# Layer 1's output projection: which matmul of the late rows is two columns wider

## The chip, the cores and the metric

One core of one Trainium2 chip runs the whole program. The metric is the device time of one execution in microseconds (us). The kernel before takes 564.82 us, the median of three runs (564.3 to 565.0).

## The reference

The model is a trunk of two layers over one sequence of 256 tokens, 1024 wide. Layer 0 mixes tokens with multi-head latent attention, layer 1 with block attention of 8 heads of 128 and a relative bias. Each mixer is followed by a dense MLP, 1024 to 4096 to 1024, with a squared ReLU. All is float32.

```
x = x + mixer(rms_norm(x, attn_norm[i]))       # ends in out @ w_o, 1024 x 1024
h = rms_norm(x, mlp_norm[i])
x = x + (relu(h @ w_in) ** 2) @ w_out
```

What the change touches is the product of the attention's result with `w_o` in layer 1. It changes no number of the output: the columns that it adds to a matmul are written to a part of a PSUM bank that nothing reads.

## The kernel before, in words

Every dense product is made of three matmuls in a row. A weight tile of 128 x 1024 float32, a *unit*, comes in by DMA (`raw`), ScalarE rounds it to a tile `wh` (line 169), and VectorE subtracts to get the rest `wl` (line 178). The activations are split the same way: `hTh` and `hTl` ahead of the MLP, `a[0]` and `a[1]` between its two products, and `aT[0]` and `aT[1]` for the heads. `mm3` (line 87) then issues three products into one PSUM bank: first `wh` with the upper half of the activations (i = 0), second `wl` with the same upper half (i = 1), third `wh` with the lower half (i = 2). In each of them the weights are the stationary 128 x 128 block and the activations are the moving 256 columns. In the trace these show as `ps<-hTh,wh`, `ps<-hTh,wl`, `ps<-hTl,wh`; for heads (`aT`) and for the second MLP product (`a`) buffer numbers are left out, so that the first and third product are both `aT,wh` or `a,wh`, and the second is `aT,wl` or `a,wl`.

`mm3` takes an argument `wide`. With it the first product of the three goes to 258 columns in place of 256. `wider` (line 103) makes the two longer access patterns; the two more columns are the first two of the next tile of activations, and they land in columns 256 and 257 of the bank, which hold nothing else. `other_type` (line 107) wraps the places inside the MLP at which matmuls of another kind stand between the products (a float32 sum over partitions, the bf16 sums of the bias tables). The next `first` or output row after such a place has a wide first product (lines 922 and 970).

`run_heads` (line 618) writes out by hand the order of one layer's attention: logits, transposes and value products of the 8 heads between the projections. Output rows 0 to 3 of `w_o` (128 output columns each) are built up head by head in `o` (line 626). Output rows 4 to 7, the late ones, are made by `col` (line 640). Row 4 is built in pieces between the heads, and its last pieces come after `o(6)` as heads 4, 5, 6 (counted from 0), then `o(7)`, then head 7; rows 5, 6, 7 follow in one go, 24 products each. Then the MLP begins: `first` (line 914) makes 8 groups of 48 products from `hTh` and `hTl`, output rows of 48 products follow, and the same again for the second half of the hidden units. `mid` is None in layer 0 and a function in layer 1; `col` uses it to tell the layers apart.

In layer 0 the wide products are those of row 4 with heads 0 and 5 (`d == 4 and h in (0, 5)`). In layer 1 there is one, that of row 5 with head 0 (`(d, h) == (5, 0)`). All of these are first products. Later in either layer's MLP there is one float32 sum over partitions inside the seventh group of 48 (line 953), after its 44th product, and the eighth group begins with a wide product. In layer 0 there are also the bias tables' sums inside the output rows; layer 1 has none.

All matmuls stand in one queue, in program order. The DMAs are issued by SyncE.

Of the kernel before, what the change touches and what calls it, by code (L numbers as in the profile page):

```python
# [18 lines left out]
P = 128  # L19
# [4 lines left out]
S = 256  # L24
NT = S // P
KD = D // P
H = 8
# [33 lines left out]
def trunk(ctx: ExitStack, tc: tile.TileContext, A, out):  # L61
# [9 lines left out]
    def ps():  # L71
        return psum.tile([P, 512], F32, name="ps", tag="ps")
# [11 lines left out]
    def mm(o, a, b, start, stop):  # L84
        nc.tensor.matmul(o, a, b, start=start, stop=stop)  # L85

    def mm3(o, a, b, start, stop, wide=None, between=None):

        for i, (w, t) in enumerate(((0, 0), (1, 0), (0, 1))):
            if wide and i == 0:  # L90
                mm(wide[0], a[w], wide[1], start, False)
            else:
                mm(o, a[w], b[t], start and i == 0, stop and i == 2)
            if between and between[0] == i:
                between[1]()
# [4 lines left out]

    moved = [True]

    def wider(bank, b):
        moved[0] = True
        return bank[:, :S + 2], flat(b[:, :2])[:, :S + 2]

    def other_type(i, f):
        def run():
# [5 lines left out]
    def flat(ap):  # L114
        return ap.rearrange("p a b -> p (a b)")
# [45 lines left out]
    def hi(n=1, eng=nc.scalar):  # L161

        for _ in range(n):
            i = len(his)
            if i < min(used[0] + RING, len(units)):
                load_raw()
                w = units[i][1]
                his.append(wsp.tile([P, 1024], F32R, name="wh", tag="wh"))
                (eng.copy if eng is nc.scalar else eng.tensor_copy)(his[i][:, :w], raws[i][:, :w])  # L169

    def lo(n=1, eng=nc.vector):

        for _ in range(n):
            i = len(los)
            if i < len(his):
                w = units[i][1]
                los.append(wsp.tile([P, 1024], F32R, name="wl", tag="wl"))
                eng.tensor_sub(los[i][:, :w], raws[i][:, :w], f32(his[i][:, :w]))  # L178
                load_raw()

    def fill(n=1):
        lo(n)
        hi(n)
# [7 lines left out]
    def unit(i):  # L191
        while len(his) <= i:
            hi()
        while len(los) <= i:
            lo()
        return his[i], los[i]

    def done(i):

        used[0] = max(used[0], i + 1)  # L200

    def part(u, sl):
        return u[0][:, sl], u[1][:, sl]
# [82 lines left out]
    class SumSquares:  # L286


        def __init__(self):
            self.tot = work.tile([P, 2, S], F32, name="ssum", tag="ssum", bufs=1)  # L290
            self.prev = None
# [38 lines left out]
    class Norm:  # L330
# [19 lines left out]
        def rows(self, tok):  # L350
            self.y = t2(self.nh, self.width)
            nc.vector.scalar_tensor_tensor(self.y, self.p.rearrange("p (a b) -> p a b", b=self.width), tok,
                                           self.rs[:, :, None].to_broadcast([P, self.nh, self.width]),
                                           op0=OP.mult, op1=OP.mult)
# [189 lines left out]
    def head_tiles(l):  # L544

        cm = ExitStack()
        pool = cm.enter_context(tc.tile_pool(name=f"heads{l}", bufs=1))
        r = []
        for c in range(2):
            r.append({n: pool.tile([P, *sh], F32, name=f"{n}{c}")  # L550
                      for n, sh in (("k", (HG, S)), ("q", (HG, S)), ("v", (NT, HG, P)))})
        room(pool, f"aT{l}")
        aT = [pool.tile([P, H, S], F32R, name=f"aT{i}") for i in range(2)]
        return cm, r, aT

    class Head:


        def __init__(self, hd, aT, h, bias, extra=None):
            self.aT = (aT[0][:, h], aT[1][:, h])  # L560
            self.two = aT[0][:, h:h + 2] if h < H - 1 else None
            self.i = h % HG
            self.hd = hd[h // HG]
            self.h, self.bias, self.extra = h, bias, extra
# [28 lines left out]
        def turn(self):  # L593
            pt = ps()
            for i in range(3):
                nc.tensor.transpose(pt[:, i * P:(i + 1) * P], self.p[:, i * P:(i + 1) * P], ident)  # L596
            self.pT = work.tile([P, 3 * P], F32, name="pT", tag="pT", bufs=3)
            nc.scalar.copy(self.pT, pt[:, :3 * P])
# [15 lines left out]
    def out_residual(a, d, gname):  # L614
        nc.vector.tensor_add(x[:, d], a, x[:, d])
        make_h_filled(d, gname)

    def run_heads(hs, proj, post, rows, turn, mid, base, gname, n1):

        A_ = [h.logits for h in hs]  # L620
        W_ = [h.weights for h in hs]
        B_ = [h.turn for h in hs]
        C_ = [h.values for h in hs]
        accs = []

        def o(h, ds=range(4)):
            u = unit(base + h // 2)
            for d in ds:
                if h == 0:
                    accs.append(ps()[:, :S])  # L630
                c = (h % 2) * 512 + d * P
                mm3(accs[d], part(u, slice(c, c + P)), hs[h].aT, h == 0, h == H - 1)
                if h == H - 1:
                    out_residual(accs[d], d, gname)
            if h % 2:
                done(base + h // 2)

        late = {}

        def col(d, hh):  # L640
            if d not in late:
                late[d] = ps()
            u = unit(base + d)
            for h in hh:

                wide = d == 4 and h in (0, 5) if mid is None else (d, h) == (5, 0)
                mm3(late[d][:, :S], part(u, slice(h * P, (h + 1) * P)), hs[h].aT, h == 0, h == H - 1,
                    wider(late[d], hs[h].two) if wide else None)
            if hh[-1] == H - 1:
                done(base + d)  # L650
                out_residual(late[d][:, :S], d, gname)

        if mid is not None:
            proj("k1", 0)
            fill(n1)
            post("k1", 0)
            mid()
            proj("k1", 1)
            lo(n1)
            rows("k1", 0)  # L660
            hi(n1)
            post("k1", 1)
        A_[0]()
        proj("v1", 0)
        if mid is not None:
            lo(n1)
            rows("k1", 1)
        W_[0]()
        hi(n1)
        post("v1", 0)  # L670
        turn("k1", 0)
        A_[1]()
        if mid is None:
            rows("k1", 1)
        B_[0]()
        proj("v1", 1)
        lo(n1 + (mid is None))
        W_[1]()
        hi(n1)
        post("v1", 1)  # L680
        turn("k1", 1)
        C_[0]()
        A_[2]()
        B_[1]()
        proj("q1", 0)
        lo(n1)
        W_[2]()
        hi(n1)
        post("q1", 0)
        C_[1]()  # L690
        A_[3]()
        B_[2]()
        proj("q1", 1)
        lo(n1)
        W_[3]()
        rows("q1", 0)
        hi(n1)
        post("q1", 1)
        C_[2]()
        B_[3]()  # L700
        o(0)
        fill()
        turn("q1", 0)
        rows("q1", 1)
        C_[3]()
        o(1)
        fill()
        turn("q1", 1)
        o(2, range(2))
        A_[4]()  # L710
        o(2, range(2, 4))
        W_[4]()
        A_[5]()
        lo()
        o(3)
        B_[4]()
        hi()
        W_[5]()
        A_[6]()
        col(4, [0, 1])  # L720
        C_[4]()
        B_[5]()
        W_[6]()
        A_[7]()
        lo()
        col(4, [2, 3])
        C_[5]()
        B_[6]()
        hi()
        W_[7]()  # L730
        o(4)
        fill()
        C_[6]()
        B_[7]()
        o(5)
        fill()
        C_[7]()
        o(6)
        fill()
        col(4, [4, 5, 6])  # L740
        o(7)
        col(4, [7])
        for d in range(5, KD):
            col(d, range(H))
# [91 lines left out]
    heads_ctx, hd, aT = head_tiles(0)  # L836
# [16 lines left out]
    for o, a, b in rope_halves(m[:, :, 0], m[:, :, 1]):  # L853
        a, b = (i[:, :, None, :].to_broadcast([P, NT, 2, HALF]) for i in (a, b))
# [46 lines left out]
    def mlp(l, base, fillers, inside, finish):  # L901

        with tc.tile_pool(name=f"mlp{l}", bufs=1) as pool:
# [10 lines left out]
            def first(b, r, j, split_k, between=None):  # L914
# [3 lines left out]
                for f, k in [(f, k) for k in range(KD) for f in range(2)] if split_k else \  # L918
                        [(f, k) for f in range(2) for k in range(KD)]:
                    c = (k % 4) * 256 + f * P  # L920
                    wide = None
                    if k == f == 0 and not moved[0]:
                        wide = wider(p[f], hTh)
                    mm3(o[f], part(u[k // 4], slice(c, c + P)), hT(k), k == 0, k == KD - 1, wide,
                        between if (f, k) == (1, KD - 2) else None)
# [326 lines left out]
```

## Time and profile before

| | us |
|---|---|
| median of three runs | 564.82 |
| the profiled execution | 564.11 |
| its span, first to last instruction | 562.3 |
| TensorE busy in it | 557.0 (99%) |
| VectorE busy | 394.7 (70%) |
| ScalarE busy | 302.4 (54%) |
| GpSimd busy | 90.5 (16%) |

The profile is of one execution. The span leaves out 1.8 us around the first and last instruction. A busy TensorE is one that has some matmul in flight: a matmul's duration as shown is 0.28 us, but the next one begins about 0.12 us after it began, so the pace has to be read from start times and not from busy time or durations. Times inside the trace are us from the start of the span.

### The profile page before, as it was taken

The page shows a single profiled execution, that of the slowest core. Times are in us where ns is not written, and L with a number is a line of the kernel's source. Part 1 is how long each engine was busy: PE and PEld are TensorE (multiplying, and loading weights), DVE is VectorE, ACT ScalarE, POOL GpSimd, SP SyncE. Part 2 cuts the span into 40 slices and gives each one's busy share as a digit, 9 for nine tenths or more (in the row PEclk, how much of TensorE's full clock was granted, in tenths as well). Part 3 has the DMA queues.
Part 4 walks back from the last instruction along what each step waited for, and adds up shares of the span by engine and source line. Part 5 has one row for each costly group of instructions (what it writes and reads, how often), then busy time and mean ns, then how long its engine had stood idle before and what let it go on. Part 6 is the DMA issues. An engine that isn't in the chain of part 4 may idle for free.

```text
span 562.3 us, 11331 instructions
## 1 busy us (share of the span) xinstructions
PE 557.0 (99%) x4612; PEld 543.8 (97%) x4612; DVE 394.7 (70%) x654; ACT 302.4 (54%) x495; POOL 90.5 (16%) x108
## 2 busy tenths in 40 slices
PE   8999999999999999999999999999999999999997
PEld 6878999999999999999999999999999999999997
DVE  5897777778997689766566657776767554777530
ACT  6899675765443355433555466756655333555310
POOL 4792100041231000011231201000211110000100
PEclk9999999999999999999999999999999999999999
DMA  8834445686566376546528344455756763765800
GB/s 300 305 113 120 144 143 160 190 273 188 191 203 207 113 223 190 188 150 194 176 82 277 119 167 145 132 170 168 268 172 195 221 187 108 219 195 155 279 26 29
DMA packets 29188, 99.60 MB, mean 177 GB/s; under 512 B 3824, under 2 KB 4720, under 8 KB 29136
## 3 DMA queue, kind: packets, MB, share of 16 engines
q1 hardware_dynamic: 28656, 97.94, 54.4%
q0 software_dynamic: 336, 0.92, 0.4%
q8 instruction: 36, 0.59, 0.4%
q14 instruction: 16, 0.13, 0.1%
q10 hardware_dynamic: 144, 0.02, 0.0%
HBM read 97.82 MB, written 1.05 MB: 176 GB/s over the span
## 4 chain that ended last, share of the span: by engine, by line
PE 96%; DVE 1%; DMA 1%; SPq 1%; issue 0%; ACT 0%; DVEq 0%
PE ps L85 93%; PE ps L372 1%; DMA x<-in_xT 1%; PE ps L596 1%; DVE wl L178 1%; SPq L158 0%; SPq L230 0%; PE ps L512 0%; DVE hTl L280 0%; ACT wh L169 0%; ACT hTh L279 0%; SPq L234 0%; DVE t L1066 0%; DVE rr L408 0%; PE ps L882 0%
## 5 line engine op out<-in xcount | busy, mean ns | idle before, releaser
L178 DVE TENSOR_TENSOR wl<-raw,wh 128x1024 fp32r<-128x1024 f32 x177 | 218.5, 1250 | 37.2 <-ACT wh L169 36.7
L169 ACT CAST wh<-raw 128x1024 fp32r<-128x1024 f32 x177 | 182.1, 1045 | 71.3 <-PE ps L85 53.6
L85 PE MATMUL ps<-a,wh 128*128 128x256 f32 x1024 | 178.5, 278 | 0.0
L85 PEld LDWEIGHTS ps<-a,wh 128*128 128x128 f32 x1024 | 155.7, 188 | 0.0
L85 PE MATMUL ps<-a,wl 128*128 128x256 f32 x512 | 143.0, 279 | 0.0
L85 PE MATMUL ps<-hTl,wh 128*128 128x256 f32 x512 | 142.7, 279 | 0.0
L85 PE MATMUL ps<-hTh,wl 128*128 128x256 f32 x512 | 142.6, 278 | 0.0
L85 PE MATMUL ps<-hTh,wh 128*128 128x256 f32 x512 | 142.4, 278 | 0.0
L85 PEld LDWEIGHTS ps<-hTh,wh 128*128 128x128 f32 x512 | 96.3, 188 | 0.1
L85 PEld LDWEIGHTS ps<-hTl,wh 128*128 128x128 f32 x512 | 96.2, 188 | 0.1
L85 PEld LDWEIGHTS ps<-a,wl 128*128 128x128 f32 x512 | 96.2, 188 | 0.0
L85 PEld LDWEIGHTS ps<-hTh,wl 128*128 128x128 f32 x512 | 96.1, 188 | 0.0
L933 ACT ACTIVATE t<-ps 128x512 f32<-128x512 f32 (+1 forms) x34 | 19.5, 573 | 66.5 <-PE ps L85 66.3
L85 PE MATMUL ps<-aT,wh 128*128 128x256 f32 x256 | 50.7, 289 | 0.0
L935 DVE SCALAR_TENSOR_TENSOR t<-ps,t 128x512 f32<-128x512 f32 (+1 forms) x34 | 22.4, 659 | 39.5 <-ACT t L933 39.5
L85 PE MATMUL ps<-wh,hTh 128*128 128x256 f32 (+2 forms) x224 | 45.7, 289 | 0.5 <-DVE wh L446 0.5
L85 PE MATMUL ps<-wl,hTh 128*128 128x256 f32 (+2 forms) x224 | 45.0, 285 | 0.4 <-DVE wl L178 0.4
L85 PE MATMUL ps<-wh,hTl 128*128 128x256 f32 (+2 forms) x224 | 45.0, 285 | 0.0
L85 PEld LDWEIGHTS ps<-aT,wh 128*128 128x128 f32 x256 | 40.5, 188 | 0.2
L85 PE MATMUL ps<-aT,wl 128*128 128x256 f32 x128 | 35.8, 280 | 0.0
L85 PEld LDWEIGHTS ps<-wh,hTh 128*128 128x128 f32 x224 | 34.4, 188 | 1.1 <-ACT hTh L279 1.0
L85 PEld LDWEIGHTS ps<-wl,hTh 128*128 128x128 f32 x224 | 34.5, 188 | 1.0 <-DVE wl L178 0.9
(167 smaller groups left out, 619.3 us busy)
## 6 DMA issues: line engine op xcount, KB each, us to landing
raw<-in_w_in_mlp SPq DMA_DIRECT2D x64, 512.0 KB, 4.3
raw<-in_w_out_mlp SPq DMA_DIRECT2D x64, 512.0 KB, 4.3
raw<-in_w_qkv SPq DMA_DIRECT2D x24, 512.0 KB, 4.2
raw<-in_w_u SPq DMA_DIRECT2D x8, 512.0 KB, 5.8
win<-in_w_in SPq DMA_DIRECT2D x8, 352.0 KB, 5.2
raw<-in_w_o0a SPq DMA_DIRECT2D x4, 512.0 KB, 3.9
raw<-in_w_o0b SPq DMA_DIRECT2D x4, 512.0 KB, 3.6
raw<-in_w_o1a SPq DMA_DIRECT2D x4, 512.0 KB, 4.2
```

Of the source, the lines that this page charges most:

```text
L85: nc.tensor.matmul(o, a, b, start=start, stop=stop)
L169: (eng.copy if eng is nc.scalar else eng.tensor_copy)(his[i][:, :w], raws[i][:, :w])
L178: eng.tensor_sub(los[i][:, :w], raws[i][:, :w], f32(his[i][:, :w]))
L372: nc.tensor.transpose(pt[:, i * P:(i + 1) * P], yf[:, i * P:(i + 1) * P], ident)
L596: nc.tensor.transpose(pt[:, i * P:(i + 1) * P], self.p[:, i * P:(i + 1) * P], ident)
L933: nc.scalar.activation(rl, src, AF.Relu)
L935: nc.vector.scalar_tensor_tensor(sq, src, 0.0, rl, op0=OP.max, op1=OP.mult)
```

## The change

`mm3` can now make any of its three products the wide one; `wider` takes the product's number. In layer 0 nothing changes. In layer 1 the wide first product of row 5 with head 0 goes back to 256 columns; row 4 gets a wide first product with head 0 and a wide third product with head 5. The wide one of head 0 begins the accumulation in the two extra columns, that of head 5 adds to them. The third product takes its moving columns from `aT[1]` (the lower half), the others from `aT[0]`.

```
     def mm3(o, a, b, start, stop, wide=None, between=None):
         for i, (w, t) in enumerate(((0, 0), (1, 0), (0, 1))):
-            if wide and i == 0:
-                mm(wide[0], a[w], wide[1], start, False)
+            if wide and i == wide[2]:
+                mm(wide[0], a[w], wide[1], start and i == 0, stop and i == 2)
             else:
                 mm(o, a[w], b[t], start and i == 0, stop and i == 2)
...
-    def wider(bank, b):
+    def wider(bank, b, which=0):
         moved[0] = True
-        return bank[:, :S + 2], flat(b[:, :2])[:, :S + 2]
+        return bank[:, :S + 2], flat(b[:, :2])[:, :S + 2], which
...
-            self.two = aT[0][:, h:h + 2] if h < H - 1 else None
+            self.two = [a[:, h:h + 2] for a in aT] if h < H - 1 else None
...
-                wide = d == 4 and h in (0, 5) if mid is None else (d, h) == (5, 0)
-                mm3(late[d][:, :S], part(u, slice(h * P, (h + 1) * P)), hs[h].aT, h == 0, h == H - 1,
-                    wider(late[d], hs[h].two) if wide else None)
+                wide = None
+                if d == 4 and h in (0, 5):
+                    which = 2 if h and mid is not None else 0
+                    wide = wider(late[d], hs[h].two[which // 2], which)
+                mm3(late[d][:, :S], part(u, slice(h * P, (h + 1) * P)), hs[h].aT, h == 0, h == H - 1, wide)
```

## Rows read from the trace of the kernel before

**Rows 1.** The page: span, and busy us, share and instructions of the engines.

```profile
span 562.3 us, 11331 instructions
...
PE 557.0 (99%) x4612; PEld 543.8 (97%) x4612; DVE 394.7 (70%) x654; ACT 302.4 (54%) x495; POOL 90.5 (16%) x108
```

**Rows 2.** Chain of waits in order of time, its end: start, us, engine, instructions.

```profile
362.96 196.15 PE ps L85 x1662
...
559.13 0.42 DVE t L1066
```

**Rows 3.** Timeline of TensorE, layer 0's late rows: start us, duration, operation, count.

```profile
82.00 0.28 PE L85 MATMUL ps<-aT,wl 128*128 128x256 f32 x1
...
82.35 0.28 PE L85 MATMUL ps<-aT,wl 128*128 128x256 f32 x1
82.47 0.40 PE L85 MATMUL ps<-aT,wh 128*128 128x256 f32 x2
82.70 0.28 PE L85 MATMUL ps<-aT,wl 128*128 128x256 f32 x1
...
83.05 0.28 PE L85 MATMUL ps<-aT,wl 128*128 128x256 f32 x1
...
130.76 0.59 PE L85 MATMUL ps<-ssum,ones 128*128 128x256 f32 x2
```

**Rows 4.** Timeline of TensorE in layer 0's MLP, 131 to 148 us.

```profile
131.31 0.28 PE L85 MATMUL ps<-hTh,wh 128*128 128x256 f32 x1
...
131.66 0.28 PE L85 MATMUL ps<-hTh,wh 128*128 128x258 f32 x1
...
147.43 0.34 PE L85 MATMUL ps<-parts,st 128*128 128x96 bf16 x4
```

**Rows 5.** Timeline of TensorE, layer 1: late rows and MLP, 355 to 559 us.

```profile
355.92 0.47 PE L85 MATMUL ps<-aT,wh 128*128 128x256 f32 x1
356.39 0.39 PE L85 MATMUL ps<-aT,wl 128*128 128x256 f32 x1
...
366.87 0.40 PE L85 MATMUL ps<-aT,wh 128*128 128x256 f32 x2
...
369.23 0.28 PE L85 MATMUL ps<-aT,wl 128*128 128x256 f32 x1
...
369.59 0.28 PE L85 MATMUL ps<-aT,wl 128*128 128x256 f32 x1
...
416.70 0.59 PE L85 MATMUL ps<-ssum,ones 128*128 128x256 f32 x2
...
417.60 0.28 PE L85 MATMUL ps<-hTh,wh 128*128 128x258 f32 x1
...
558.81 0.28 PE L85 MATMUL ps<-a,wh 128*128 128x256 f32 x1
```

**Rows 6.** Line 85 from 81 to 82.58 us: durations min/median/max in ns.

```profile
L85 PEld LDWEIGHTS ps<-aT,wl x5: 187/188/193, 80.8 to 82.2; 128*128 128x128 f32 x5
L85 PE MATMUL ps<-aT,wl x5: 280/281/281, 80.9 to 82.3; 128*128 128x256 f32 x5
```

**Rows 7.** The same from 378 to 416 us, where the three products have three names.

```profile
L85 PE MATMUL ps<-hTh,wh x108: 279/281/281, 377.9 to 415.8; 128*128 128x256 f32 x108
L85 PEld LDWEIGHTS ps<-hTh,wl x108: 186/187/188, 378.0 to 415.8; 128*128 128x128 f32 x108
...
L85 PEld LDWEIGHTS ps<-hTl,wh x108: 187/188/189, 378.1 to 415.9; 128*128 128x128 f32 x108
```

**Rows 8.** The same from 365 to 369 us.

```profile
L85 PEld LDWEIGHTS ps<-aT,wl x12: 186/187/192, 364.9 to 368.8; 128*128 128x128 f32 x12
```

**Rows 9.** The same from 450 to 558 us.

```profile
L85 PE MATMUL ps<-hTh,wl x128: 279/281/281, 468.6 to 513.5; 128*128 128x256 f32 x128
```

**Rows 10.** Busy time by stretch: PE, PEld, DVE, ACT, POOL; clock, DMA share, GB/s.

```profile
84.00:130.00 46.00, 46.00 (x409) 46.00 (x408) 34.71 (x48) 29.81 (x43) 7.28 (x7) 1.00 0.64 205
...
450.00:500.00 50.00, 50.00 (x427) 50.00 (x426) 30.80 (x35) 22.05 (x27) 2.95 (x4) 1.00 0.58 177
```

## The prediction

> **What bounds the kernel now.** I read the engines' shares first: TensorE is busy 99% of the span, the next engine (VectorE) 70% [rows 1]. The chain of waits comes second, read at its end: one unbroken piece of TensorE, 196.15 us and 1662 matmuls long from 362.96 us, and behind it a last addition and the store [rows 2]. So from 363 us on nothing sets the end but how fast TensorE goes from one matmul to the next. The change lies at the head of that piece. The third view is the timeline of TensorE, and it has to be read by starts. In layer 0 the second products (`aT,wl`) of neighbouring groups of three start at 82.00 and 82.35 us, and a little later at 82.70 and 83.05; over a long stretch one sees two different paces:
>
> - *Fast*: from 82.70 us to the sum at 130.76 us there are by the code 2 + 3 products (row 4's heads 5 and 6), 12 (`o(7)`), 3 (row 4's head 7), 72 (rows 5 to 7), 6 x 48 and 44 of the MLP, so 424 starts: 48.06 us / 424 = 113.4 ns [rows 3]. From the wide product at 131.66 to the bias sums at 147.43 us there are 48 + 48 + 43 = 139: 15.77 / 139 = 113.5 ns [rows 4].
> - *Slow*: from the third product of row 4's head 5, the first of the two in the row of 366.87, to the sum at 416.70 there are 1 + 3 + 12 + 3 + 72 (row 4's rest, `o(7)`, rows 5 to 7), 288 and 44, so 423: 49.83 / 423 = 117.8 ns. From 417.60 to the last matmul at 558.81 there are 48 + 8 x 48 + 8 x 48 + 8 x 48 - 1 = 1199: 141.21 / 1199 = 117.8 ns [rows 5].
>
> The shape is the same 128 x 256 everywhere, the granted clock is 1.00 in both layers, and TensorE never sits idle in either [rows 10]. Layer 0's MLP runs at 113.4 ns, layer 1's at 117.8 ns, and nothing in the arithmetic asks for it.
>
> **What switches the pace.** In layer 0 the two matmuls in the row of 82.47 are the third product of row 4's head 4 and the wide first product of head 5. Up to it groups of three are 0.35 to 0.36 us apart; from 82.70 on 113.4 ns is held over 48 us, through the late rows and into the MLP [rows 3]. The wide product at 131.66, behind the float32 sum, is again followed by the fast pace, while the three starts just ahead of it, from 131.31, took 0.35 us [rows 4]. In layer 1 the wide product of row 5, 19 starts behind that of 366.87 and so at 369.1 us, is followed by the slow pace; so is the one at 417.60 [rows 5]. So a wide product can lift the pace, and sometimes doesn't.
>
> The line view says when. In the slow pace the three products of a group aren't alike. From 378 to 416 us one has the longest weight load (up to 189 ns: `hTl,wh`, the third), the next one the longest matmul (median 281: `hTh,wh`, the first), the one after it the shortest load (median 187, from 186: `hTh,wl`, the second) [rows 7]. This order of three can begin at any product: from 450 to 558 us the median of 281 is on `hTh,wl` [rows 9]. In layer 0, just before the wide product that works, the second product carries the 281 and loads of 188 [rows 6]; so the one before it, the first, carries the long load, and there the wide one sits. In layer 1, ahead of the wide one that fails, the second carries the load of 187 [rows 8]; so the third carries the long load, and the wide one sits on the first, a step too late. My reading: two more columns lift the pace when they fall on the product of the long load. The change moves them in layer 1 to a third product of that same stretch.
>
> **The change part by part.**
>
> - *Row 4, head 0, wide first product.* Two more columns: by TensorE's pace of 113.4 ns for 256 columns under 1 ns, and the matmul it falls on is followed by a start 0.47 us later, where 0.12 is usual (355.92 to 356.39) [rows 5]. It waits there for its `wl`, so the columns are covered; without that cover they cost 1 ns. Nothing else comes of it: a wait and three heads' transposes stand between it and the last stretch.
> - *Row 5, head 0, wide product removed.* Back to 256 columns: under 1 ns.
> - *Row 4, head 5, wide third product.* Under 1 ns itself. If it lifts the pace, 423 starts, from 366.87 to 416.70, go at 113.4 ns: 49.83 - 423 x 0.1134 = 49.83 - 47.97 = 1.86 us less.
> - *The sum at 416.70 and the wide first product at 417.60.* Neither is edited. The sum drops the pace in layer 0 too (0.35 us for three starts from 131.31 [rows 4]), and there the same order of matmuls, which came in at the fast pace, is lifted by its wide product at 131.66. Layer 1 came in slow. If it now comes in fast, I take it to be lifted as layer 0 is: 141.21 - 1199 x 0.1134 = 141.21 - 135.97 = 5.24 us less.
> - *What a faster TensorE asks of the others.* Weights must come 4% sooner. Layer 0's MLP does that with the same tiles: at the fast pace DVE 34.71, ACT 29.81 of 46 us and 205 GB/s, no idle time of TensorE; layer 1's 450 to 500 has less to do (30.80, 22.05 of 50 us) [rows 10]. The last matmul to the end of the span, 3.5 us (558.81 to 562.3), stays.
>
> No instruction, DMA or wait is added or moved past a queue; only three matmuls change their columns. What the trace doesn't show is a wide third product. Below, it can do what the failing one of row 5 did: nothing that lasts, and one group of 0.36 us behind it (369.23 to 369.59) in place of 0.353 [rows 5], which rival 4 prices. Above, what the working ones did: 7.10 us. I take the upper end, since it stands on the product on which the working one stood.
>
> Sum: 1.86 + 5.24 = 7.10 us. The profiled execution took 564.11, so 557.0 for it; the median of the runs shown is 0.7 above that execution, so 557.7 for a median. I forecast 557.6.
>
> **A rule of the Trainium skill against it.** *TensorE: Matmul & The Clock Gate*, "Back-to-back issue gap", gives the isolated gap of a warm matmul by its columns alone, N/2.4 + 2.5 ns; by it 256 columns take 109.2 ns, two more 0.8, and the change is worth nothing: 564.8. This trace disagrees, with 113.4 and 117.8 ns at one shape and one clock. The same section says that in a stream the spacing comes from load and matmul together; the rows agree, but it doesn't say which pace one gets.
>
> **Rivals.**
>
> 1. *The columns lift nothing in layer 1.* Then both stretches stay at 117.8 ns: 564.8. Either they cost their columns alone and layer 0's fast pace has another reason (against it: the pace turns at both wide products of rows 3 and 4, within a group). Or the order of the three is another one in the changed kernel, so that the third product is the wrong one. For it: the order can begin at any product. Against: the stretch behind the last transposes has the same matmuls as before up to the wide one, and from 365 to 416 us the second product kept the short load [rows 7, 8].
> 2. *The first lifts, the second doesn't.* The pace falls at the sum and stays: 564.8 - 1.9 = 562.9. For it: 417.60 failed before. Against: layer 0's twin.
> 3. *The first fails, the second happens to lift* from another order: 564.8 - 5.2 = 559.6. It needs a shift that nothing here calls for.
> 4. *Slower: the wide product puts the stream on a third, slower pace.* Behind the failing wide product one group takes 0.36 us, 120 ns a start, 2.2 more than the slow pace (369.23 to 369.59) [rows 5]. Held over 423 + 1199 starts it would cost 1622 x 2.2 = 3.6 us: 568.4. It decides from 0.7 ns a start over these 1622, which is 1.1 us. Against: over the 1199 starts behind 417.60 the mean is 117.8, so no such pace lasted there.
>
> **How the numbers follow.** Forecast 0.70, rival 1 0.16 (0.04 by its first cause, 0.12 by its second), rival 2 0.07, rival 3 0.03, rival 4 0.04. The forecast's own range is 556.6 to 558.6 (the spread of the runs, 0.7, and some 0.3 for the entries into the pace). For 8 in 10 the range takes in rivals 3 and 2: 556.4 to 563.2. A measurement of this kernel can tell 0.2% (1.1 us) from no change. Faster by more: 0.70 + 0.07 + 0.03 = 0.80; within: 0.16; slower: 0.04.
>
> **What would show it.** In the profile after, second products behind 367.1 us 0.34 us apart in place of 0.353; the sum at about 414.8 in place of 416.70; the wide product behind it followed by 113.4 ns; the three products alike in load and duration, where a 281 and a 187 stood out; the last matmul at about 551.7; no idle time of TensorE in between. I am wrong if the sum still comes at 416.7 (the order or the mechanism), or comes early and the MLP behind it goes on at 117.8 ns (the second lift).

## The result, and the profile after

The changed kernel takes 557.46 us, the median of four runs (557.23 to 557.75), against 564.57 of the kernel before: a ratio of 0.9874, with a 95% interval of 0.9857 to 0.9891. 557.6 was forecast.

The page's head for the profiled execution, which took 557.23 us (answers to [rows 1]):

```profile
span 555.5 us, 11331 instructions
...
PE 550.2 (99%) x4612; PEld 536.6 (97%) x4612; DVE 395.2 (71%) x654; ACT 302.4 (54%) x495; POOL 91.0 (16%) x108
```

The same number of instructions, TensorE still at 99%. The end of the chain of waits in order of time (answers to [rows 2]):

```profile
363.27 188.95 PE ps L85 x1662
...
552.25 0.42 DVE t L1068
```

The one unbroken piece of TensorE has the same 1662 matmuls and is 188.95 us long, not 196.15: 7.20 us less. The whole difference lies in it. The two profiled executions are only 6.88 us apart because this one is 0.32 us late before anything that changed: the wide product of row 4, head 0 starts at 356.24 where it stood at 355.92 [rows 5].

The timeline of TensorE around the change and behind it (start, duration, operation, count; answers to [rows 5]; in a merged row the shape is that of its first matmul):

```profile
356.24 0.47 PE L85 MATMUL ps<-aT,wh 128*128 128x258 f32 x1
356.72 0.39 PE L85 MATMUL ps<-aT,wl 128*128 128x256 f32 x1
...
366.71 0.28 PE L85 MATMUL ps<-aT,wl 128*128 128x256 f32 x1
...
367.07 0.28 PE L85 MATMUL ps<-aT,wl 128*128 128x256 f32 x1
367.19 0.40 PE L85 MATMUL ps<-aT,wh 128*128 128x258 f32 x2
367.42 0.28 PE L85 MATMUL ps<-aT,wl 128*128 128x256 f32 x1
...
367.76 0.28 PE L85 MATMUL ps<-aT,wl 128*128 128x256 f32 x1
...
415.14 0.59 PE L85 MATMUL ps<-ssum,ones 128*128 128x256 f32 x2
...
416.04 0.28 PE L85 MATMUL ps<-hTh,wh 128*128 128x258 f32 x1
...
551.93 0.28 PE L85 MATMUL ps<-a,wh 128*128 128x256 f32 x1
```

Second products are 0.36 us apart ahead of the wide third product at 367.19 (366.71 to 367.07) and 0.34 behind it (367.42 to 367.76). From it to the sum the 423 starts take 47.95 us, 113.4 ns each, where they took 49.83. From the wide product behind the sum to the last matmul the 1199 starts take 135.89 us, 113.3 ns each, where they took 141.21. These are 1.88 and 5.32 us, together 7.20.

Line 85 just ahead of the wide product (365.5 to 367.1 us) and behind it (378 to 414), durations in ns as min/median/max (answer to [rows 8] and [rows 7]):

```profile
L85 PE MATMUL ps<-aT,wl x6: 279/279/279, 365.3 to 367.1; 128*128 128x256 f32 x6
L85 PEld LDWEIGHTS ps<-aT,wl x5: 187/187/187, 365.5 to 367.0; 128*128 128x128 f32 x5
```

```profile
L85 PE MATMUL ps<-hTl,wh x107: 276/276/276, 377.7 to 413.8; 128*128 128x256 f32 x107
L85 PE MATMUL ps<-hTh,wh x107: 276/276/276, 377.8 to 413.9; 128*128 128x256 f32 x107
...
L85 PE MATMUL ps<-hTh,wl x106: 276/276/276, 378.0 to 413.7; 128*128 128x256 f32 x106
```

Ahead of it the second product still has the short load of 187, as in [rows 8], so the wide one did fall on the product of the long load. Behind it all three products are alike, 276. (In this profile and most that follow, durations read up to 1 ns below those of the rows of before, so "280 and 188" here is the "281 and 189" there.) What the others had to deliver they delivered, with TensorE never idle (a stretch of [rows 10]):

```profile
450.00:500.00 50.00, 50.00 (x443) 50.00 (x443) 32.48 (x38) 23.31 (x28) 2.34 (x4) 1.00 0.59 183
```

### The profile page after: what moved, and what is told of

Read it like the earlier page. It is cut to its first block, busy times and chain, and to the rows that moved or that the text cites. A ratio compares the mean times of both kernels' runs of the same rounds, so it can differ in the third digit from the quotient of the medians.

```text
span 555.5 us, 11331 instructions
## 1 busy us (share of the span) xinstructions
PE 550.2 (99%) x4612; PEld 536.6 (97%) x4612; DVE 395.2 (71%) x654; ACT 302.4 (54%) x495; POOL 91.0 (16%) x108
## 4 chain that ended last, share of the span: by engine, by line
PE 96%; POOL 2%; DMA 1%; SPq 1%; issue 0%; DVE 0%
PE ps L85 93%; PE ps L372 2%; PE ps L596 1%; DMA rowp<-in_rowp 1%; POOL gsc L425 0%; SPq L158 0%; POOL pr L410 0%; SPq L230 0%; POOL ang L393 0%; POOL rr L411 0%; PE ps L512 0%; POOL rr L415 0%; POOL kk L403 0%; POOL posf L391 0%; DVE t L1068 0%
## 5 line engine op out<-in xcount | busy, mean ns | idle before, releaser
L85 PE MATMUL ps<-a,wh 128*128 128x256 f32 x1024 | 175.0, 276 | 0.0
L85 PE MATMUL ps<-aT,wh 128*128 128x256 f32 (+1 forms) x256 | 50.2, 288 | 0.0
L85 PEld LDWEIGHTS ps<-wh,hTl 128*128 128x128 f32 x224 | 34.7, 188 | 0.8 <-DVE hTl L280 0.8
```

## The experiments

Eleven kernels ran; each is given with the kernel before as it ran on the same chip.

| run | us | before | ratio, 95% interval |
|---|---|---|---|
| e1: first product wide | 564.52 | 564.41 | 1.0003, 0.9993 to 1.0012 |
| e2: second product wide | 559.21 | 564.41 | 0.9905, 0.9888 to 0.9921 |
| e3: third product, head 4 | 557.33 | 564.41 | 0.9876, 0.9861 to 0.9890 |
| e4: MLP's wide one moved | 557.40 | 564.41 | 0.9875, 0.9861 to 0.9890 |
| e4b: no wide one in the MLP | 562.35 | 564.59 | 0.9962, 0.9947 to 0.9977 |
| e5: before, and one more in the MLP | 559.27 | 564.59 | 0.9907, 0.9892 to 0.9922 |
| e6: four columns, third product | 559.32 | 564.59 | 0.9906, 0.9892 to 0.9921 |
| e7: four columns, first product | 558.83 | 564.59 | 0.9900, 0.9883 to 0.9916 |
| e8: four columns, second product | 559.31 | 564.40 | 0.9909, 0.9895 to 0.9924 |
| e9: MLP tiles 224 bytes lower | 564.02 | 564.40 | 0.9993, 0.9984 to 1.0003 |
| e10: MLP tiles 64 lower, 256 higher | 563.14 | 564.43 | 0.9977, 0.9968 to 0.9987 |

**e1, e2, e3: which product.** Each differs from the changed kernel in one place of `col`.

```
e1 -                    which = 2 if h and mid is not None else 0
   +                    which = 0
e2 +                    which = 1 if h and mid is not None else 0
e3 -                if d == 4 and h in (0, 5):
   +                if d == 4 and h in (0, 5 if mid is None else 4):
```

> The changed kernel, but in layer 1 the wide product of row 4, head 5 is the first of its three and not the third. Theory (the two columns lift the pace only on the product of the long weight load, in this stretch the third): no lift at 367 us, and none at the sum behind it since the stream comes in slow as before: 564.6. Rival A (any wide product at this place lifts; row 4 and the wide product of head 0 are what counts): 557.5, as the changed kernel.

> The changed kernel, but in layer 1 the wide product of row 4, head 5 is the second of its three. Theory: the second is the product of the short load here, so no lift at 367 us; 564.6, or 559.3 if the failed one turns the order so that the wide product behind the sum lifts. Rival A (any wide product at this place lifts): 557.5.

> The changed kernel, with the wide third product three products earlier, at row 4, head 4. Theory: the order of the three repeats with each group, so the third product of head 4 has the long load as well: lifts, 557.4 (3 starts sooner, 0.01 us). Rival B (a particular place or address works, and the change was lucky): 564.6 or 562.7.

Measured: 564.52, 559.21 and 557.33. The same columns at the same row and head are worth nothing on the first product, 5.2 us on the second and 7.1 on the third; and they are worth 7.1 on the third of the head before. So it isn't the place (rival A) nor luck with one address (rival B), but the product. Nor is it the third product as such: in layer 0 [rows 3] and in e5 below it is a wide first product that lifts. e1 also carries the change's two other edits (row 4's head 0, row 5's head 0), which by themselves are worth nothing. e2 is the more telling one. Line 85 between the wide product and the sum, first in e1, then in e2:

```profile
L85 PE MATMUL ps<-hTh,wh x105: 280/280/280, 378.0 to 414.8; 128*128 128x256 f32 x105
L85 PEld LDWEIGHTS ps<-hTh,wl x105: 187/187/187, 378.0 to 414.8; 128*128 128x128 f32 x105
...
L85 PEld LDWEIGHTS ps<-hTl,wh x105: 188/188/188, 378.2 to 414.9; 128*128 128x128 f32 x105
```

```profile
L85 PEld LDWEIGHTS ps<-hTh,wh x105: 187/187/187, 378.1 to 414.9; 128*128 128x128 f32 x105
...
L85 PEld LDWEIGHTS ps<-hTh,wl x105: 188/188/188, 378.3 to 415.0; 128*128 128x128 f32 x105
...
L85 PE MATMUL ps<-hTl,wh x104: 280/280/280, 378.5 to 414.9; 128*128 128x256 f32 x104
```

Both are slow. In e1 the order is that of the kernel before [rows 7]: long load on the third product, 280 on the first, short load on the second. In e2 it has moved back by one: long load on the second. Two columns on the product of the short load therefore turn the order without lifting the pace. The stream then meets the sum in another order, and the MLP's wide product, the same instruction as in e1, lifts. The last matmuls and loads ahead of it tell the two cases apart, first in the kernel before (at 417.5 us), then in e2 (at 418.2 us):

```profile
L85 PE MATMUL ps<-hTl,wh x1: 281/281/281, 417.5 to 417.5; 128*128 128x256 f32 x1
L85 PEld LDWEIGHTS ps<-hTh,wh x1: 187/187/187, 417.5 to 417.5; 128*128 128x128 f32 x1
```

```profile
L85 PE MATMUL ps<-hTh,wl x1: 280/280/280, 418.0 to 418.0; 128*128 128x256 f32 x1
L85 PEld LDWEIGHTS ps<-hTl,wh x1: 187/187/187, 418.0 to 418.0; 128*128 128x128 f32 x1
```

In the kernel before the longest matmul behind the sum is on the third product and the short load on the wide product itself: the two columns lift nothing and turn the order back by one, as in e2's late rows (the 281 of [rows 9] is on the second). In e2 the longest is on the second and the short load on the third, so the wide product is the one of the long load. So the same reading covers this wide product too: it lifts where the order behind the sum puts the long load on it. These are single matmuls, 1 to 3 ns apart, but the other traces agree: in the changed kernel and in e6 to e8 the longest of the three matmuls ahead of it is the second, in e1 and e5, where it misses, the third. Its rows in e2:

```profile
418.13 0.28 PE L85 MATMUL ps<-hTl,wh 128*128 128x256 f32 x1
418.25 0.28 PE L85 MATMUL ps<-hTh,wh 128*128 128x258 f32 x1
...
418.60 0.28 PE L85 MATMUL ps<-hTh,wh 128*128 128x256 f32 x1
...
418.83 0.28 PE L85 MATMUL ps<-hTl,wh 128*128 128x256 f32 x1
```

From 418.60 to 418.83 two starts take 0.23 us and the pace stays: 559.21 is the kernel before less 5.2.

**e4, e4b: the second term by itself.** e4 forbids the wide first product of `first` in layer 1. e4b forbids all in layer 1's MLP.

```
e4  -                    if k == f == 0 and not moved[0]:
    +                    if k == f == 0 and not moved[0] and l == 0:
e4b (in first)
    +                if l == 1:
    +                    moved[0] = True
    (and in the output rows)
    -                            wider(bank, a[0]) if f == 0 and not moved[0] else None,
    +                            wider(bank, a[0]) if f == 0 and not moved[0] and l == 0 else None,
```

> The changed kernel without layer 1's second wide product, the one behind the float32 sum in the MLP. Theory: the first lift stays until the sum (1.9 us), the sum drops the pace, and nothing lifts it again: 557.5 + 5.3 = 562.8. Rival C (the pace comes back by itself or the sum doesn't drop it): 557.5.

> The changed kernel with no wide product anywhere in layer 1's MLP (in the run before this one the wide product had only moved to the first output row, 48 products later). Theory: the first lift holds to the sum and saves 1.9 us, the sum drops the pace, and the 1199 starts behind it stay slow: 557.5 + 5.3 = 562.7. Rival C (the pace comes back by itself): 557.5.

e4 took 557.40 where I expected 562.8: a miss, but of my edit. `moved` stayed False, so the next place that looks at it, the first output row, made the wide product:

```profile
421.61 0.28 PE L85 MATMUL ps<-a,wh 128*128 128x258 f32 x1
```

It stands 48 products later and lifts there; 48 slow starts more are 0.2 us, too little to be told. e4b did what was meant, and took 562.35. Its timeline:

```profile
414.67 0.28 PE L85 MATMUL ps<-hTh,wl 128*128 128x256 f32 x1
414.79 0.59 PE L85 MATMUL ps<-ssum,ones 128*128 128x256 f32 x2
...
415.34 0.28 PE L85 MATMUL ps<-hTh,wh 128*128 128x256 f32 x1
...
415.69 0.28 PE L85 MATMUL ps<-hTh,wh 128*128 128x256 f32 x1
...
556.91 0.28 PE L85 MATMUL ps<-a,wh 128*128 128x256 f32 x1
```

The sum drops the pace (0.35 us for three starts from 415.34). From 415.69 on 1199 starts take 141.22 us, 117.8 ns: without a wide product the pace doesn't come back by itself (rival C). So the first lift alone is worth 564.59 - 562.35 = 2.2 us by the medians (1.9 by the sum), and the second the rest.

**e5: the kernel before, lifted elsewhere.** If the rule holds, it should place a wide product where none was tried. In the kernel before the long load is on the first product from 418 us on (the 281 of [rows 9] is on the second). e5 makes the first product of the MLP's first output row wide.

```
-                            wider(bank, a[0]) if f == 0 and not moved[0] else None,
+                            wider(bank, a[0]) if f == 0 and (not moved[0] or (l, r, d) == (1, 0, 0)) else None,
```

> The kernel before with one more wide product: the first of layer 1's first output row in the MLP (second product a, 48 products behind the wide one that failed). In the profile of the kernel before the long load is on the first product from 418 us on, since the failed one turned the order. Theory: this one falls on the long load and lifts the last 1151 starts: 1151 x 4.4 ns = 5.1 us, 559.4. Rival D (in layer 1's MLP the pace can't be lifted once the stream came in slow; it needs the lift in the late rows): 564.5.

Measured: 559.27. The order ahead of it and the matmuls from it to the end:

```profile
L85 PE MATMUL ps<-hTh,wl x15: 280/280/280, 418.9 to 423.9; 128*128 128x256 f32 x15
L85 PEld LDWEIGHTS ps<-hTl,wh x15: 187/187/187, 418.9 to 423.9; 128*128 128x128 f32 x15
```

```profile
424.11 0.28 PE L85 MATMUL ps<-a,wh 128*128 128x258 f32 x1
...
554.57 0.28 PE L85 MATMUL ps<-a,wh 128*128 128x256 f32 x1
```

1151 starts in 130.46 us, 113.3 ns. A stream that came in slow can be lifted (against rival D).

**e6, e7, e8: four columns in place of two.** In `wider` `S + 2` becomes `S + n`, and layer 1's row 4 asks for n = 4, with head 0 and with head 5; at head 5 e6 does so on the third product, e7 on the first, e8 on the second.

```
-        return bank[:, :S + 2], flat(b[:, :2])[:, :S + 2], which
+        return bank[:, :S + n], flat(b[:, :2])[:, :S + n], which
```

> The changed kernel with four more columns in place of two in layer 1's row 4 (heads 0 and 5). Theory (which product counts, not how many columns): lifts, 557.5. Rival E (the columns push the stream by steps, and two steps from the long load lead elsewhere): no lift at 367 us, 564.5, or 559.3 where it turns the order.

> Four more columns on the first product of row 4, head 5 in layer 1 (two of them failed there, 564.5). Theory (which product counts): 564.5. Rival E (steps): four columns may do on another product what two do on the long load: 557.5, or 559.3 where it turns the order.

> Four more columns on the second product of row 4, head 5 in layer 1, the one of the short load (two more turned the order there by one product and lifted nothing by themselves: 559.2). Theory (each column is a push of fixed size, and only some sizes on some products lead out of the slow order): no firm call whether this one does; 557.5 if it lifts, and if not, what the order on arrival at the sum says: long load on the third product there, then the MLP's wide product misses and it is 564.5; on the first or second, then it hits and it is 559.2. Rival A (which product counts, not how many columns): 559.2, and the order as in the run with two.

Measured: 559.32, 558.83, 559.31. My theory as it stood ("which product counts, not how many columns") fell with e6 and e7: four columns on the product of the long load don't lift (559.32 where 557.5 was expected), and four on the first product do what two didn't (558.83 where 564.5 was expected). Line 85 from 378 to 415 us in e6, e7 and e8:

```profile
L85 PE MATMUL ps<-hTl,wh x106: 280/280/280, 377.9 to 415.0; 128*128 128x256 f32 x106
L85 PEld LDWEIGHTS ps<-hTh,wh x106: 187/187/187, 377.9 to 415.0; 128*128 128x128 f32 x106
```

```profile
L85 PE MATMUL ps<-hTh,wl x105: 280/280/280, 377.9 to 414.7; 128*128 128x256 f32 x105
L85 PEld LDWEIGHTS ps<-hTl,wh x105: 187/187/187, 377.9 to 414.7; 128*128 128x128 f32 x105
```

```profile
L85 PE MATMUL ps<-hTh,wl x105: 280/280/280, 378.2 to 415.0; 128*128 128x256 f32 x105
L85 PEld LDWEIGHTS ps<-hTl,wh x105: 187/187/187, 378.2 to 415.0; 128*128 128x128 f32 x105
```

All three are slow there, and all three have turned the order: the long load, one ahead of the 280, has gone from the third product to the second in e6 and to the first in e7 and e8. In all three the MLP's wide product then lifts. For e8 no firm call had been made: what was said beforehand is that an order with the long load on the first or second product at the sum goes with 559.2, and it does. Rival A gave e8 the same time, but the order of e2 (long load on the second), and that isn't what came. In sum, of six trials in the late rows (two or four columns on each product) one lifts at once (two on the long load), one does nothing (two on the product behind it), and four turn the order. The wide product behind the sum misses when the long load arrives on the third product (before, e1, e5) and lifts when it arrives on the second (e2, e6) or first (e7, e8), or when the stream arrives fast.

**e9, e10: where the tiles lie.** No instruction changes; the padding (`ROOM`) ahead of the MLP's tiles `a[0]`, `a[1]` does.

```
     "a0": 224, "a1": 224      (kernel before, and changed)
e9   "a0": 224, "a1": 0
e10  "a0": 160, "a1": 480
```

> The changed kernel with the 224 bytes of padding ahead of layer 1's MLP tiles a[0] and a[1] taken away, so that both lie 224 bytes lower; no instruction is another one. Theory F (the fast pace rests on how the moving tiles lie against the weight tiles): the 768 products of the MLP's second half, and what is left behind them, lose the fast pace: at 4.4 ns each 3.4 to 5.2 us, 560.9 to 562.7. Rival G (the pace is a matter of the order in time alone): 557.5.

> The changed kernel with other paddings ahead of the MLP tiles a[0] and a[1]: 160 bytes in layer 0 and 480 in layer 1 in place of 224, so that they lie 64 bytes lower and 256 bytes higher; no instruction is another one. With 224 bytes lower the products from these tiles took 120 ns a start. Theory F (the pace of a stretch rests on how its moving tiles lie against its weights): each layer's products from a[0], a[1] show a pace of their own, in steps to be read; where it is 120 ns as with 224 lower, 768 x 6.7 ns = 5.1 us are lost in that layer, and what follows on it. A pace under 113.3 ns would be a gain of 768 times the difference. Theory G (only the one shift of 224 is bad): 557.5.

Measured: 564.02 and 563.14. First layer 1's products from `a` in e9, by durations and by the starts of the first of them and of the first product behind them, then layer 0's in e10 (64 bytes lower), then layer 1's in e10 (256 higher):

```profile
L85 PE MATMUL ps<-a,wl x112: 279/282/286, 424.9 to 464.8; 128*128 128x256 f32 x112
```

```profile
421.51 0.28 PE L85 MATMUL ps<-a,wh 128*128 128x256 f32 x1
...
467.58 0.28 PE L85 MATMUL ps<-hTh,wh 128*128 128x256 f32 x1
```

```profile
L85 PEld LDWEIGHTS ps<-a,wh x151: 188/192/193, 149.9 to 176.9; 128*128 128x128 f32 x151
L85 PE MATMUL ps<-a,wl x76: 281/283/284, 149.9 to 176.9; 128*128 128x256 f32 x76
```

```profile
L85 PE MATMUL ps<-a,wl x111: 276/276/277, 427.5 to 464.9; 128*128 128x256 f32 x111
```

In e9 384 starts take 46.07 us: 120.0 ns each, worse than the slow pace, and nearly all of the change's gain is gone, though both wide products lifted (the sum stood at 415.16, and the 48 starts from the MLP's wide product to 421.51 took 5.45 us). 564.02 lies above the 560.9 to 562.7 that I expected, which had taken the slow pace, 4.4 ns a start more, where it was 6.7; and the 384 products from `hTh` and `hTl` that stand between two lots of 384 from `a`, and whose own tiles didn't move, went on at the slow pace, 117.8 ns (467.58 to 512.81). In e10's layer 0 it is 27.0 / (75 x 3) = 120.0 ns, with loads of 192, while layer 1, 256 bytes higher, keeps 276 and the fast pace; 563.14 is 5.7 us above the changed kernel, the 5.1 that I expected for layer 0 and some more. So where the moving tiles lie sets the pace of a stretch (theory F), and G (the order in time alone, or only the one shift) is wrong. Theory F's other half, that it is how they lie against the weights, is not shown: no run moved the weights.

No run beats the changed kernel: e3's 557.33 and e4's 557.40 are within its spread.

## Why the prediction was right

- *What bounds it.* TensorE's pace behind 363 us was the whole bound; the piece shrank by 7.20 us and the end with it. The sum came at 415.14 and the last matmul at 551.93, 0.3 and 0.2 us behind the forecast places, in an execution that was 0.32 us late from the start.
- *Which product.* The wide one was said to lift on the product of the long load, read from three durations 1 to 2 ns apart. e1, e2, e3 and e5 bear that out for two columns, e5 at a place chosen by the rule alone. For four columns it doesn't hold (e6).
- *First term, 1.86 us.* Measured 1.88 in the trace.
- *Second term, 5.24 us.* Measured 5.32 in the trace; e4b, without it, is 4.9 us behind the changed kernel by the medians. Its reason was too narrow: I took the MLP's wide product to lift because the stream would arrive fast, as in layer 0. It also lifts for a stream that arrives slow in another order (e2, e6 to e8); what it needs is the order behind the sum that puts the long load on it, and a fast arrival is one way to that order.
- *Wide product of head 0, nothing.* It starts 0.48 us ahead of its successor (356.24 to 356.72), against 0.47 without the columns: covered by the wait for `wl`.
- *A faster TensorE's needs.* Met, with no idle time.
- *The rivals.* The columns' own cost alone (rival 1's first cause) is ruled out by e1 against the changed kernel: as many columns, 7.1 us apart. Its second cause didn't come about. The first lift without the second (rival 2) came only where e4b left the second wide product out: 562.35, against the 562.9 worked out. Rival 3's course, the first lift missed and the second made, is what e2 took when made to, at 559.2 against the 559.6 worked out. No third pace (rival 4) came from a wide product; it came from moved tiles.

The Trainium skill (*TensorE: Matmul & The Clock Gate*, "Back-to-back issue gap") gives an isolated gap by columns alone; by its formula that is an estimate of 109.2 ns for 256. No stretch of these runs meets it; 113.3, 117.8 and 120.0 ns appear at one shape and at a granted clock of 1.00.

The kernel before has two more wide products in layer 1, in its projections, where the activations are the stationary block; the prediction doesn't read them. They start at 272.04 and 282.97 us. Starts are about 0.118 us apart ahead of both and 0.113 to 0.114 soon behind them, so wide products lifted the pace in layer 1 before the change too. At 272.04 the longest load, 193 ns, is the wide product's own; at 282.97 it isn't, but that of the product behind (the wide one's load is the first of these):

```profile
L85 PEld LDWEIGHTS ps<-wh,hTl x1: 187/187/187, 282.9 to 282.9; 128*128 128x128 f32 x1
L85 PEld LDWEIGHTS ps<-wh,hTh x1: 192/192/192, 283.0 to 283.0; 128*128 128x128 f32 x1
```

So the reading by the long load is borne out in the late rows and the MLP, and not for every stream of loads and matmuls.

Not settled: what in the chip makes the two paces and the order of three, and why four columns do other than two. The runs show that the pace turns on two more columns at one product, and on where the moving tiles lie; no run here shows the cause of either. Nor was a wide third product of row 5 tried alone.

## What to carry to other kernels

When the same matmul shape runs at two paces in two parts of a kernel bound by TensorE, read start times over hundreds of matmuls and durations by product, since a busy share of 99% and equal clocks hide a 4% difference. A stream of load and matmul pairs can sit in a slower order for 1199 starts, which two more columns at the right matmul end at once; a wide product that fails at one place in the group of three is to be tried on its neighbours before it is given up, and the state is checked again behind each matmul of another kind. Before that, the padding ahead of the moving tiles is worth a trial of its own: here 64 bytes in one layer cost 5.7 us (e10, 563.14 against 557.46).

## What was not expected

- Four columns do less than two at the right product, and more than two at the product behind it (e6, e7): how many columns are added counts as well as where.
- A wide product that lifts nothing can still pay 50 us later, by the order in which the stream meets the next matmul of another kind (e2: 5.2 us).
- Products from tiles 64 bytes lower (layer 0) or 224 lower (layer 1) take 120.0 ns a start; 256 higher (layer 1) the pace stays at 113.3 (e9, e10).
